# Two transformer blocks on one core: filler matmuls in the routings, one more weight slot, a reordered last expert and later lambda steps

## The chip, the core and the metric

The kernel runs on one core of a Trainium2 chip, as one program. The metric is the device time of that program in microseconds (us). The core's engines, each with a queue of its own, are TensorE (PE, matmuls; PEld is its loading of weights), VectorE (DVE), ScalarE (ACT), GpSimd (POOL) and SyncE (SP), which issues most transfers. All transfers share 16 DMA engines.

## The reference

The input is one sequence of 256 tokens of width 1024, in f32. Block 1 scales and shifts a normalised x by vectors made from a condition (six of them, `cond @ ada_w`), mixes tokens with differential attention (8 heads, each the difference of two softmaxes, weighted by a number lambda), and adds a mixture of 16 experts. Block 2 conditions x in the same way, mixes tokens with a sparse attention (scores of an index choose keys by top-k) and an RWKV recurrence side by side, and adds a mixture of 32 experts. Cut to what the change touches:

```python
lam = exp(sum(lam_q1 * lam_k1)) - exp(sum(lam_q2 * lam_k2)) + lam_init
a = softmax(s1) - lam * softmax(s2)
...
g_idx = argmax(t @ w_rg + b_rg)                 # one group of experts per token
top_v, top_i = top_k(e_logits[g_idx], 2)        # two experts in it
hid = silu(t @ w_gate) * (t @ w_up) * gates     # for each expert
y = hid @ w_down
...
x = block2(block1(x))
```

Every expert has 1024 x 512 weights for gate and up and 512 x 1024 for down, 6 MB per expert, all of which are read.

## The kernel before, in words

Activations are held in on-chip memory with features on the partitions (`xT`, eight blocks of 128 features x 256 tokens). Large buffers come from a pool of 1 MB units, `c.un` (`raw()` takes one, `give()` returns it). Weights arrive through a `Stream` (L98): each `get` or `load` takes the oldest of its slots and issues one transfer of 1 MB on SP's queue; `size(n)` and `grow()` set how many units serve as slots. A transfer waits on SP until its slot has been read, and at most eight are in flight. SP's queue is in order, so a step that waits on it holds all later loads.

The text is written stage by stage; a scheduler then sets the order of instructions on every engine by its own estimates, and where the text says `keep_in_program_order`, it leaves an instruction's place. Stretches in which several chains run side by side (`weave`, L137) take steps from each in turn.

The stages, with the parts the change touches:

- **First projections and attention of block 1.** `load_late` (L212) brings four vectors of 64, and on DVE makes the product `lp` (L220) and its sums `ls` (L222), on ACT their exponential (L223), on DVE lambda (L226, L227). L405 is the product with the condition weights `ada_w`, `rsx` (L1363) a copy that PE waits for, L738 a copy in the attention.
- **Output projection and router.** `Project.rest` (L913) finishes the four quarters q of an output projection; each quarter gives two feature blocks of xT, by L926 on DVE. When a block is ready, `each(fb)` calls `Tokens.block` (L944), which transposes it to rows of tokens in the accumulator `acc` (L953 or L955), and multiplies it with the router's weights (L957). After blocks 3 and 7 ACT squares half of the rows and sums them (L961). `Tokens.rstd` (L963) adds the sums (L967) and finds 1/rms.
- **Routing.** `Route.slots` scales the logits, picks the group and two experts on DVE (L1042 to L1060) and ranks the tokens of each expert with small matmuls (L1063 to L1065). `count` (L1086, L1087) and `flag` (L1092, L1094) give `rfl`, whether an expert has more tokens than its place holds (64 in block 1, 32 in block 2). `Tokens.high` and `low` (L978, L986) round the rows to two parts.
- **Dispatch and experts.** `dispatch` (L1113 on, matmul L1135) gathers the tokens of a few experts. `experts` (L1254) loops over the experts: gate and up (L1213), the previous expert's `back()`, its down projection (L1222), gate factor and rounding (L1193 to L1197), and `add`, which scatters the result into `acc` (L1239 in block 1, L1249 in block 2). `slots_T` makes the scatter matrix, `hidden` the hidden layer (L1151 to L1163). The last expert is split in two halves q of columns (matmul L1297). `at` names steps that are done ahead of an expert: `general` (`overflow`, L1302 on) contains the path for more tokens than fit. It reads the flag into registers (L1309) and branches (L1310); the branch is not taken with these inputs. In both blocks it stands ahead of expert 1, and afterwards returns the unit `c.uxT` that it would need.
- **End.** `end(q)` (L2237) copies half q of `acc` on DVE and ACT and sends it to the output from SP and ACT.
- **Between the blocks**, block 2 copies `acc` to xT (L2079) and squares it (L2080). In block 2, L1644 and L1648 make the first products of the recurrence, L1915 and L1916 the top-k, L2003 and L2004 the attention's scores; L624 is the low part of a rounding; L719 turns a row of factors that L1937 spreads.

## Time and profile before

| what | us |
|---|---|
| median of three timed runs | 1311.84 |
| lowest and highest | 1310.52, 1313.15 |
| profiled execution | 1314.67 |
| its span | 1313.1 |
| PE, PEld busy | 1120.9 (85%), 684.6 (52%) |
| DVE, ACT, POOL busy | 587.0 (45%), 345.1 (26%), 101.9 (8%) |
| mean granted clock of PE | 0.94 |

The experts of block 1 lie between about 246 and 490 us, those of block 2 between about 857 and the end. Busy times are sums over the span; a share says nothing of whether an engine sets the end in a stage. An entry in brackets behind an instruction is the idle time of its engine just before it, with what ended it; the granted clock is the share of full speed that PE was given.

### The profile page before, as it was taken

The numbers are of one execution on the slowest core, as the hardware profiler recorded it, in microseconds if no ns is written. First come the engines' busy times: TensorE is split into PE (matmuls) and PEld (weight loads), VectorE is DVE, ScalarE is ACT, GpSimd is POOL, SyncE is SP. The second block draws the span as 40 slices with busy tenths as digits, with TensorE's granted clock in tenths as the row PEclk, the third lists the DMA queues.
The fourth block names the chain that finished last, engine by engine and source line by source line (L and its number), as shares of the span: only waits on it lengthen the run. The fifth ranks groups of instructions, "written<-read, shape, count | busy, mean of one in ns | idle before, by whom it ended". The sixth has DMA issues, their size and how long they took to land. (4 is left out here: it accounts for less than half of the span.)

```text
span 1313.1 us, 19778 instructions
## 1 busy us (share of the span) xinstructions
PE 1120.9 (85%) x8050; PEld 684.6 (52%) x8050; DVE 587.0 (45%) x1435; ACT 345.1 (26%) x676; POOL 101.9 (8%) x115
## 2 busy tenths in 40 slices
PE   5899978799999987988899999799877786787775
PEld 2777768444444335886678779744322232232222
DVE  4568762423222237677676767443322132222112
ACT  3334441212111114552334324222211121111111
POOL 2521110100000004001410100000000000000000
PEclk7899987799999995998999999899998899989988
DMA  8777767699999912332055588679999999999995
GB/s 301 292 263 266 293 267 287 257 411 422 422 421 420 421 66 74 149 128 97 33 169 194 186 317 306 243 304 421 421 423 422 421 422 422 421 422 422 422 421 240
DMA packets 60513, 404.04 MB, mean 308 GB/s; under 512 B 7328, under 2 KB 7584, under 8 KB 14464
## 3 DMA queue, kind: packets, MB, share of 16 engines
q1 hardware_dynamic: 58464, 400.58, 76.1%
q10 hardware_dynamic: 1824, 2.00, 0.5%
q8 instruction: 65, 1.06, 0.3%
q0 software_dynamic: 128, 0.13, 0.2%
q14 instruction: 32, 0.26, 0.1%
HBM read 401.64 MB, written 1.05 MB: 307 GB/s over the span
## 5 line engine op out<-in xcount | busy, mean ns | idle before, releaser
L1213 PE MATMUL a<-u,u 128*32 128x512 f32 (+1 forms) x1480 | 288.4, 610 | 38.8 <-DMA u<-in_expert_w_up 24.8
L1193 DVE SCALAR_TENSOR_TENSOR gs<-a,gc,gt 128x512 f32<-128x512 f32 (+1 forms) x50 | 37.6, 751 | 377.2 <-PE a L1222 366.4
L1213 PEld LDWEIGHTS a<-u,u 128*32 128x32 f32 (+1 forms) x1480 | 70.9, 120 | 181.6 <-issue 113.9
L1222 PE MATMUL a<-u,hid 128*32 128x512 f32 (+1 forms) x704 | 127.4, 622 | 36.7 <-DMA u<-in_expert_w_down 36.7
L679 PE MATMUL a<-u,u 128*128 128x256 f32 x656 | 142.9, 295 | 2.6 <-DVE u L624 2.6
L679 PE MATMUL a<-u,hi 128*128 128x256 f32 x640 | 136.9, 305 | 0.4 <-ACT u L1528 0.4
L1151 ACT COPY gs<-a 128x512 f32<-128x512 f32 x48 | 28.1, 585 | 337.0 <-PE a L1213 337.0
L679 PEld LDWEIGHTS a<-u,u 128*128 128x128 f32 x656 | 106.0, 196 | 12.6 <-issue 9.2
L1195 ACT CAST u<-gs 64x512 fp32r<-64x512 f32 x96 | 59.2, 616 | 198.9 <-DVE gs L1193 197.8
L679 PEld LDWEIGHTS a<-u,hi 128*128 128x128 f32 x640 | 101.0, 194 | 14.7 <-issue 9.3
L1222 PEld LDWEIGHTS a<-u,hid 128*32 128x32 f32 (+1 forms) x704 | 31.2, 119 | 112.2 <-issue 45.2
L1197 DVE TENSOR_TENSOR u<-gs,u 64x512 fp32r<-64x512 f32 x96 | 65.9, 686 | 27.2 <-ACT u L1195 25.3
L624 DVE TENSOR_TENSOR u<-u,hi 128x1024 fp32r<-128x1024 f32 x48 | 63.6, 1332 | 15.4 <-ACT hi L623 15.1
L623 ACT CAST hi<-u 128x1024 fp32r<-128x1024 f32 x48 | 49.8, 1047 | 75.0 <-PE a L679 68.8
L903 PE MATMUL a<-u,u 128*128 128x256 f32 x256 | 48.1, 307 | 6.6 <-DVE u L624 5.8
L624 POOL TENSOR_TENSOR u<-u,u 128x512 fp32r<-128x512 f32 (+1 forms) x22 | 43.1, 1975 | 135.1 <-ACT u L623 135.1
L1180 DVE CAST PT<-a 128x256 fp32r<-128x256 f32 x48 | 20.4, 424 | 63.2 <-PE a L1178 38.3
L1249 PE MATMUL acc<-u,PT 128*128 128x512 f32 x128 | 43.9, 456 | 5.2 <-DVE u L1197 3.6
L457 DVE SCALAR_TENSOR_TENSOR mvsum<-u,cond_c,mvsum 128x512 f32<-128x512 f32 x56 | 43.0, 768 | 11.6 <-DMA u<-in_ada_w 10.9
L1158 PEld LDWEIGHTS a<-sel,gs 128*128 128x128 f32 x256 | 34.3, 208 | 26.5 <-issue 25.5
L758 PE MATMUL e<-u,u 128*128 128x256 f32 x288 | 40.4, 307 | 5.5 <-ACT u L586 5.0
L623 ACT CAST u<-u 128x512 fp32r<-128x512 f32 (+1 forms) x52 | 40.9, 830 | 15.2 <-PE a L903 7.3
(445 smaller groups left out, 1555.1 us busy)
## 6 DMA issues: line engine op xcount, KB each, us to landing
u<-in_expert_w_up SPq DMA_DIRECT2D x93, 1024.0 KB, 19.7
u<-in_expert_w_gate SPq DMA_DIRECT2D x92, 1024.0 KB, 19.8
u<-in_expert_w_down SPq DMA_DIRECT2D x92, 1024.0 KB, 19.7
u<-in_ada_w SPq DMA_DIRECT2D x32, 1024.0 KB, 6.6
u<-in_w_in SPq DMA_DIRECT2D x19, 1024.0 KB, 4.8
u<-in_ada_w SPq DMA_DIRECT2D x32, 512.0 KB, 4.0
u<-in_attn_w_in SPq DMA_DIRECT2D x12, 512.0 KB, 8.7
u<-in_attn_w_in SPq DMA_DIRECT2D x6, 1024.0 KB, 7.0
```

What stands on the lines that cost most here:

```text
L457: V.scalar_tensor_tensor(out=mine[0], in0=w[:, k], scalar=cs[:, k:k + 1], in1=mine[0], op0=ALU.mult, op1=ALU.add)
L623: nc.scalar.copy(h[:, o], w[:, o])
L624: (nc.vector if e == "v" else nc.gpsimd).tensor_tensor(l[:, o], w[:, o], h[:, o].bitcast(F32), ALU.subtract)
L679: c.nc.tensor.matmul(ps, a[:, k, c0:c0 + n], b[:, k], start=k == 0 and i == 0, stop=k == kn - 1 and i == 2)
L758: T.matmul(p[:, j * S:(j + 1) * S], l, r, start=(h, j, k, n) == (0, 0, 0, 0), stop=(h, k, n) == (1, 3, 2), skip_group_check=True)
L903: self.c.nc.tensor.matmul(ps[:, j * S:(j + 1) * S], a[:, k, j * P:(j + 1) * P], b[:, k], start=k + j + i == 0, stop=k == KD - 1 and i == 2 ...
L1193: c.nc.vector.scalar_tensor_tensor(out=y[o], in0=py[o], scalar=gc[o], in1=gt[o], op0=ALU.mult, op1=ALU.mult)
L1195: c.nc.scalar.copy(yy[H2[q], q], y[H2[q]])
L1197: c.nc.vector.tensor_tensor(yy[H2[1 - q], q], y[H2[q]], yy[H2[q], q].bitcast(F32), ALU.subtract)
L1213: c.nc.tensor.matmul(pg[r:r + cap], xe[:, k0 + k, x0:x0 + cap], w[:, k, :], start=k0 + k < nk, stop=k0 + k >= KD - nk)
L1222: c.nc.tensor.matmul(py[r:r + cap], hT[:, f], w[:, f - f0, q * 512:(q + 1) * 512], start=f < nk, stop=f >= 4 - nk)
L1249: c.nc.tensor.matmul(acc[:, 2 * t + q], PT[:, t * P:(t + 1) * P], yy[:, q], start=False, stop=stop, skip_group_check=True)
```

## The change

- Lambda's product, sum and exponential are placed by the program's order.
- `rest` hands over blocks 4 and 5 in the middle of the last quarter's projection.
- `acc` becomes four tiles of one bank each. The squares of the second half are done in two parts, after blocks 5 and 7.
- `rstd` issues six matmuls, 128x512 in f32, whose result nobody reads.
- In block 2, `uxT` is given before the slots grow; `general` stands ahead of expert 30, and takes a slot back for `uxT`; ahead of expert 31 four slots are taken for the output copies.
- With `early`, expert 31's hidden layer comes before expert 30's return, and both halves' last matmuls before the adds of the halves.

```diff
@@ load_late
-    nc.vector.tensor_tensor(lp, lm[:, 0:2], lm[:, 2:4], ALU.mult)
+    own(nc.vector.tensor_tensor(lp, lm[:, 0:2], lm[:, 2:4], ALU.mult))
...
-    nc.vector.tensor_reduce(ls, lp, AX.X, ALU.add)
-    nc.scalar.activation(ls, ls, AF.Exp)
+    own(nc.vector.tensor_reduce(ls, lp, AX.X, ALU.add))
+    own(nc.scalar.activation(ls, ls, AF.Exp))
@@ Project.rest
-                run(self.part(q, ps, w, 0, 8))
+                run(self.part(q, ps, w, 0, 4))
+                for fb in (4, 5) if q == 3 else ():
+                    each(fb)
+                run(self.part(q, ps, w, 4, 8))
...
-            for fb in ((), (), (0, 1, 2, 3), (4, 5))[q]:
+            for fb in (0, 1, 2, 3) if q == 2 else ():
                 each(fb)
@@ Tokens.block
-            o = self.acc[:, 2 * t + q, k % 4 * P:(k % 4 + 1) * P]
+            o = self.acc[2 * t + q][:, k % 4 * P:(k % 4 + 1) * P]
...
-        if k % 4 == 3:
+        if k in (3, 5, 7):
+            o = slice(0, 512) if k == 3 else slice(0, 256) if k == 5 else slice(256, 512)
             for t in range(2):
-                c.nc.scalar.activation(self.u[:, :512], self.acc[:, 2 * t + q], AF.Square, accum_out=self.ss[:, t, q:q + 1])
+                c.nc.scalar.activation(self.u[:, o], self.acc[2 * t + q][:, o], AF.Square,
+                                       accum_out=self.ss[:, t, k // 2 - 1:k // 2])
@@ Tokens.rstd
-        V.tensor_tensor(v, self.ss[:, :, 0], self.ss[:, :, 1], ALU.add)
+
+        ps = bank(c)
+        for _ in range(6):
+            c.nc.tensor.matmul(ps, c.ones, self.u[:, :512], start=True, stop=True)
+        V.tensor_reduce(v.unsqueeze(2), self.ss, AX.X, ALU.add)
@@ experts
-        if hid is not None:
+        if hid is not None and not (early and e == NE - 1):
             out = back()
         PT, gc = slots_T(c, ep, slot[:, :, e:e + 1], gate[:, :, e:e + 1], cap)
-        hid = e, hidden(c, ep, pg, cap), PT, gc
+        hT = hidden(c, ep, pg, cap)
+        if early and e == NE - 1:
+            out = back()
+        hid = e, hT, PT, gc
...
-    add(*out)
+    if not early:
+        add(*out)
...
+    def last(q):
+        add(ys[q], PT, True, (q,))
+        end(q)
     for q in range(2):
...
-        add(gated(c, ep, py, gc, gt, (q,)), PT, True, (q,))
-        end(q)
+        if q:
+            c.ys.reverse()
+        ys.append(gated(c, ep, py, gc, gt, (q,)))
+        if not early:
+            last(q)
+    if early:
+        add(*out)
+        last(0)
+        last(1)
@@ block 1 and block 2
-    acc = c.e1.enter_context(tc.tile_pool(name="accp", bufs=1, space=PSUM)).tile([P, 4, 512], F32, name="acc")
+    acc = four_banks(c.e1.enter_context(tc.tile_pool(name="accp", bufs=1, space=PSUM)))
...
+def four_banks(pool):
+    return [pool.tile([P, 512], F32, name=f"acc{i}") for i in range(4)]
...
+        un.give(c.uxT)
         st.grow()
...
         def general():
+            st.size(len(st.slots) - 1)
+            c.uxT = un.raw()
             overflow(c, ep, fl_, "_2", 32, 32, (th_, tl_), slot, gate, add, c.gt2)
-            un.give(c.uxT)
-            st.grow()
...
-                f = c.xe[:, 512 * (2 * q + t):512 * (2 * q + t + 1)]
-                copy(f, acc[:, 2 * t + q])
+                f = c.un.raw()[:, :512]
+                copy(f, acc[2 * t + q])
                 dma.dma_start(out[0, t * P:(t + 1) * P, q * 512:(q + 1) * 512], f)
-        experts(c, "y", 32, (th_, tl_), slot, gate, add, 32, ep, c.gt2, {1: general}, end)
+        experts(c, "y", 32, (th_, tl_), slot, gate, add, 32, ep, c.gt2, {30: general, 31: lambda: st.size(len(st.slots) - 4)}, end, True)
```

The changed program's lines are shifted: its L960 and L962 are L955 and L957 of before, L977 are the six new matmuls, L1074 is L1063, L1233 is L1222, L1260 is L1249, L1318 is L1297, L1337 is L1309, L1672 is L1644, L721 is L719, L1965 is L1937.

In the following pieces rows that repeat the one ahead of them are left out. SP's queue at the start of block 2's experts, before: `xu` and `u` are slots, `rfl` is the flag.

```order
L128 DMA xu_7132<-in_expert_w_gate 128x2048 [waits DMASW0_49,SP_sequencer_49,DMASW1_49,DVE_sequencer_49,DMASW2_49,PE_sequencer_49,DMASW3_49,Activation_sequencer_49,DMAHW1_49,Pool_sequencer_49,PE_49]
L128 DMA u_7269<-in_expert_w_gate 128x2048 [waits DMAHW2_49,PE_49]
L128 DMA u_7270<-in_expert_w_up 128x2048 [waits DMAHW3_49,DVE_49]
L1309 TENSOR_LOAD rfl_7265 [waits PE_49,DVE_49,Activation_49,Pool_49]
L1309 ISA x2
L128 DMA xu_7132<-in_expert_w_gate 128x2048 [waits DMAHW4_49,DMAHW1_49,PE_49]
L128 DMA u_6849<-in_expert_w_up 128x2048 [waits DMAHW5_49,PE_49]
L1310 COMPARE_AND_BRANCH
```

And with the change:

```order
L128 DMA xu_7149<-in_expert_w_gate 128x2048 [waits DMASW0_49,SP_sequencer_49,DMASW1_49,DVE_sequencer_49,DMASW2_49,PE_sequencer_49,DMASW3_49,Activation_sequencer_49,DMAHW1_49,Pool_sequencer_49,PE_49]
L128 DMA u_7293<-in_expert_w_gate 128x2048 [waits DMAHW2_49,PE_49]
L128 DMA u_7295<-in_expert_w_gate 128x2048 [waits DMAHW3_49,DVE_49,PE_49]
L128 DMA u_7294<-in_expert_w_up 128x2048 [waits DMAHW4_49,DVE_49,PE_49]
L1337 TENSOR_LOAD rfl_7289 [waits PE_49,DVE_49,Activation_49,Pool_49]
L1337 ISA x2
L128 DMA xu_7149<-in_expert_w_up 128x2048 [waits DMAHW5_49,DMAHW1_49,PE_49]
```

Four loads stand ahead of the flag where three stood; the branch has left this place, and comes 160 rows later, with twelve loads behind it.

PE at the end of the program, before: `hid` is an expert's hidden layer, `PT` a scatter matrix.

```order
L1222 MATMUL a<-u_7270,hid 32x512 [waits DMAHW6_49,DVE_49]
L1222 MATMUL a<-xu_7132,hid 32x512 [waits DMAHW7_49]
L1158 MATMUL a<-sel,gs 128x64 [waits Activation_49]
L1249 MATMUL acc<-u_7267,PT 128x512 [waits DVE_49]
L1249 MATMUL acc<-u_7267,PT 128x512 [waits DVE_49]
L1297 MATMUL a<-u_6849,hid 32x512 [waits DMAHW0_49,DVE_49]
L1297 MATMUL a<-u_6850,hid 32x512 [waits DMAHW1_49,PE_49]
L1249 MATMUL acc<-u_7267,PT 128x512 [waits DVE_49]
L1249 MATMUL acc<-u_7267,PT 128x512 [waits Activation_49]
```

And with the change, where `acc` has four numbers:

```order
L1169 MATMUL a<-sel,gs 128x64 [waits Activation_49]
L1233 MATMUL a<-u_6866,hid 32x512 [waits DMAHW6_49,DVE_49,PE_49]
L1233 MATMUL a<-u_6867,hid 32x512 [waits DMAHW7_49]
L1318 MATMUL a<-u_6868,hid 32x512 [waits DMAHW0_49,DVE_49]
L1260 MATMUL acc_6723<-u_7291,PT 128x512 [waits DVE_49]
L1260 MATMUL acc_6724<-u_7291,PT 128x512 [waits DVE_49]
L1318 MATMUL a<-u_6869,hid 32x512 [waits DMAHW1_49]
L1260 MATMUL acc_6723<-u_7291,PT 128x512 [waits DVE_49]
L1260 MATMUL acc_6724<-u_7291,PT 128x512 [waits DVE_49]
```

The hidden layer of expert 31 (L1169, L1158 before) has moved ahead of expert 30's down projection, the scatters of expert 30 stand between the two halves, and the last scatter no longer waits for ACT.

PE in block 2, before: `b<-` are the first products of the recurrence, `grows` and L2003 belong to the attention.

```order
L719 MATMUL a<-ident,u_2728 128x128 [waits DVE_49]
L679 MATMUL a<-u_3690,hi_3806 128x256
L1644 MATMUL b<-u_4672,u_4403 64x128 x2
L1937 MATMUL a<-grows_4706,u_2728 128x256 [waits Activation_49]
L2003 MATMUL a<-u_3928 128x128 [waits DVE_49]
L1644 MATMUL b<-u_4672,u_4403 64x128 x7
L2003 MATMUL a<-u_3928 128x256 [waits DVE_49] x2
L1644 MATMUL b<-u_4672,u_4403 64x128 x15
L2019 MATMUL a<-ident,u_4156 128x128 [waits Pool_49] x2
```

And with the change:

```order
L681 MATMUL a<-u_3701,u_3817 128x256
L1672 MATMUL b<-u_4684,u_4415 64x128 [waits DVE_49]
L1672 MATMUL b<-u_4684,u_4415 64x128 x31
L721 MATMUL a<-ident,u_2740 128x128 [waits DVE_49]
L1965 MATMUL a<-grows_4718,u_2740 128x256 [waits Activation_49]
L681 MATMUL a<-u_3701,hi_3818 128x256 [waits PE_49]
```

The 32 products stand in one block ahead of the attention's factors.

## Rows read from the trace of the kernel before

**Rows 1.** Windows: us; busy (count) of PE, PEld, DVE, ACT, POOL; PEclk, DMA share, GB/s.

```profile
275.00:300.00 25.00, 24.88 (x143) 12.72 (x140) 7.75 (x19) 4.98 (x9) 0.00 (x0) 1.00 1.01 422
950.00:975.00 25.00, 18.38 (x122) 6.95 (x116) 6.78 (x16) 3.61 (x7) 0.00 (x0) 1.00 1.01 422
```

**Rows 2.** Chain that ended last, block 2's experts: start, duration, what.

```profile
938.46 1.97 PE a L1135 x16
...
1274.70 19.75 DMA xu<-in_expert_w_down
```

**Rows 3.** Timeline of the first projections: start, duration, engine, line, operation.

```profile
19.10 0.29 DVE L220 TENSOR_TENSOR lp<-lm 128x128 f32<-128x128 f32 x1 [5.63 <-DMA lm<-in_attn_lam_k]
...
20.10 3.64 PE L405 MATMUL a<-u,cond_c 128*32 128x512 f32 x16 [3.91 <-DVE rsx L1363]
...
20.95 0.20 PEld L405 LDWEIGHTS a<-u,cond_c 128*32 128x32 f32 x4 [0.66 <-DMA u<-in_ada_w]
```

**Rows 4.** Windows of 2 us in both routings, columns as in rows 1.

```profile
228.00:230.00 2.00, 0.00 (x0) 0.00 (x0) 1.29 (x8) 0.43 (x2) 0.00 (x0) 1.00 0.50 205
...
238.00:240.00 2.00, 2.00 (x12) 2.00 (x11) 2.00 (x6) 0.00 (x0) 0.00 (x0) 0.50 0.04 8
...
848.00:850.00 2.00, 0.01 (x1) 0.05 (x1) 1.76 (x15) 1.57 (x4) 0.00 (x0) 0.50 0.03 8
```

**Rows 5.** Timeline of the first routing and its dispatch.

```profile
224.90 0.88 DVE L926 SCALAR_TENSOR_TENSOR u<-a,mod,u 128x256 f32<-128x256 f32 x2 [7.61 <-PE a L903]
...
227.03 0.60 ACT L961 ACTIVATE u<-acc 128x512 f32<-128x512 f32 x1 [8.21 <-PE acc L955]
...
228.46 0.16 DVE L967 TENSOR_TENSOR tv<-u 128x2 f32<-128x2 f32 x1 [2.69 <-ACT u L961]
...
234.01 0.61 PE L1063 MATMUL a<-rA,tri 128*128 128x16 f32 x2 [6.73 <-DVE rA L1060]
...
237.02 5.86 PE L1135 MATMUL a<-pm,u 128*128 128x256 f32 x32 [0.69 <-DVE pm L1120]
...
237.12 2.72 DVE L986 SCALAR_TENSOR_TENSOR u<-acc,ty,u 128x512 fp32r<-128x512 f32 x4
...
242.71 3.60 PE L1447 MATMUL acc<-u,ident 128*128 128x512 f32 x8
```

**Rows 6.** Timeline of the second routing and its dispatch.

```profile
849.99 0.61 PE L1063 MATMUL a<-rA,tri 128*128 128x32 f32 x2 [7.77 <-DVE rA L1060]
...
852.42 2.72 DVE L986 SCALAR_TENSOR_TENSOR u<-acc,ty,u 128x512 fp32r<-128x512 f32 x4
...
855.90 1.49 DVE L1142 TENSOR_SCALAR u<-a,A2b,mod 128x256 f32<-128x256 f32 x3 [0.76 <-PE a L1135]
...
857.89 0.14 DVE L1094 TENSOR_SCALAR rfl<-rcm 128x1 int32<-128x1 f32 x1
...
861.15 0.33 SPq L128 DMA_DIRECT2D xu<-in_expert_w_gate  x1
```

**Rows 7.** Timeline of the program's end.

```profile
1299.19 3.74 PE L1297 MATMUL a<-u,hid 128*32 128x512 f32 x16
...
1305.13 0.74 PE L1249 MATMUL acc<-u,PT 128*128 128x512 f32 x2 [2.20 <-DVE u L1197]
...
1306.64 0.58 ACT L2237 COPY u<-acc 128x512 f32<-128x512 f32 x1 [1.57 <-DVE u L2237]
...
1307.27 1.22 PE L1249 MATMUL acc<-u,PT 128*128 128x512 f32 x2 [1.40 <-ACT u L2237]
...
1309.94 0.35 ACTq L2238 DMA_DIRECT2D out<-u  x1
```

**Rows 8.** Timeline of the block boundary, VectorE's first copies.

```profile
491.49 2.48 DVE L2079 COPY u<-acc 128x512 f32<-128x512 f32 x4 [0.59 <-PE acc L1239]
```

**Rows 9.** Timeline of block 2 before its attention's scores.

```profile
631.13 1.10 PE L1644 MATMUL b<-u,u 64*64 64x128 f32 x30
...
633.13 0.75 DVE L1648 TENSOR_TENSOR u<-b,u 128x256 f32<-128x256 f32 x2
```

More of the change, by code (lines that the diff above doesn't have):

```diff
@@ L218, in load_late @@
         nc.gpsimd.dma_start(lm[:, i, :], I[nm].partition_broadcast(P))
+    own = c.tc.keep_in_program_order
     lp = tp.tile([P, 2, 64], F32, name="lp")
-    nc.vector.tensor_tensor(lp, lm[:, 0:2], lm[:, 2:4], ALU.mult)
+    own(nc.vector.tensor_tensor(lp, lm[:, 0:2], lm[:, 2:4], ALU.mult))
     ls = tp.tile([P, 2], F32, name="ls")
-    nc.vector.tensor_reduce(ls, lp, AX.X, ALU.add)
-    nc.scalar.activation(ls, ls, AF.Exp)
+    own(nc.vector.tensor_reduce(ls, lp, AX.X, ALU.add))
+    own(nc.scalar.activation(ls, ls, AF.Exp))
     c.lam = cp.tile([P, 1], F32, name="lam")
@@ L941, in __init__ @@
         self.u = c.un.raw()
-        self.ss = self.u[:, 512:516].rearrange("p (t q) -> p t q", t=2)
+        self.ss = self.u[:, 512:518].rearrange("p (t q) -> p t q", t=2)
     def block(self, k):
@@ L1238, in add @@
                 fb = 4 * q + b
-                c.nc.tensor.matmul(acc[:, fb // 2, (fb % 2) * S:(fb % 2 + 1) * S], yy[:, q, b * P:(b + 1) * P], PT,
+                c.nc.tensor.matmul(acc[fb // 2][:, (fb % 2) * S:(fb % 2 + 1) * S], yy[:, q, b * P:(b + 1) * P], PT,
                                    start=False, stop=stop, skip_group_check=True)
@@ L1248, in add, with experts @@
             for t in range(2):
-                c.nc.tensor.matmul(acc[:, 2 * t + q], PT[:, t * P:(t + 1) * P], yy[:, q],
+                c.nc.tensor.matmul(acc[2 * t + q], PT[:, t * P:(t + 1) * P], yy[:, q],
                                    start=False, stop=stop, skip_group_check=True)
     return add
-def experts(c, pfx, NE, tok, slot, gate, add, cap, ep, gt, at={}, end=lambda q: None):
+def experts(c, pfx, NE, tok, slot, gate, add, cap, ep, gt, at={}, end=lambda q: None, early=False):
     nc, st = c.nc, c.st
@@ L1446, in block1 @@
         for b in range(4):
-            nc.tensor.matmul(acc[:, b], c.ident, fl(xT[:, 2 * b:2 * b + 2]), start=True, stop=False, skip_group_check=True)
+            nc.tensor.matmul(acc[b], c.ident, fl(xT[:, 2 * b:2 * b + 2]), start=True, stop=False, skip_group_check=True)
         split_rows(c)
@@ L1456, in block1 @@
         un.give(uoh, uol, c.uys, c.xe)
-    return acc.rearrange("p a (b s) -> p (a b) s", b=2)
+    return acc
 def lin_block(c, name, x, sink):
@@ L2186, in block2 @@
         pl = stack.enter_context(tc.tile_pool(name="pl2", bufs=1, space=PSUM))
-        acc = stack.enter_context(tc.tile_pool(name="accp2", bufs=1, space=PSUM)).tile([P, 4, 512], F32, name="acc")
+        acc = four_banks(stack.enter_context(tc.tile_pool(name="accp2", bufs=1, space=PSUM)))
         c.banks.append((pe, 1))
```

7 lines of the change are left out of this document (4 added, 3 removed).

## The prediction, made before the changed kernel ran

> **What bounds the kernel now.** I read the table of windows first, for the limit of each stage. In [rows 1] the experts of block 1 show TensorE (PE) busy 24.88 of 25 us, so the sixteen experts are bound by PE; those of block 2 show PE busy 18.38 of 25, yet DMA share 1.01 at 422 GB/s: the thirty-two are bound by weight loading. A step is therefore judged by its stage: before 863 us by the instruction chain, afterwards by when the weight stream starts and how soon the output leaves once the stream has ended.
>
> The chain of waits agrees: up to the end of the last experts it hops from load to load, [rows 2] being one, 19.75 us from issue to landing; since eight are in flight, one load lands every 19.75 / 8 = 2.47 us. The other row there is a dispatch in the middle of these experts: 16 matmuls in 1.97 us, 0.123 us each. That is the price at the higher of TensorE's two clock levels, 2.4 GHz; both routings pay more, below.
>
> **The change part by part.** The sum is made against the profiled execution (1314.67 us, span 1313.1). It stands 2.83 us above the median 1311.84 of the three timed runs, so the changes are taken off the median.
>
> *Lambda's first steps, -0.3.* The product `lp` sat on VectorE (DVE) until lambda's vectors had landed, 5.63 us idle, and only then came the copy `rsx`, for which PE waited 3.91 us [rows 3]. Now `rsx` goes first. Not all of the 3.91 returns: PE's second group of weights arrives at 20.95 in any case [rows 3], and the work after it, half of 3.64 us, would end near 22.9 instead of 23.74: -0.8. Lambda's two large steps (0.29 us for the row shown, the second as long by estimate) go into the attention, among DVE's work there; I charge +0.5, bounds 0 and +0.9. No DMA moves with them.
>
> *Fillers in both routings.* While DVE finds experts, PE idles 6.73 us in the first routing and 7.77 in the second [rows 5, 6]. The granted clock falls during it, from 1.00 to 0.50, and is still 0.50 while the dispatch runs [rows 4]: 32 matmuls in 5.86 us, 0.183 each [rows 5]. The six extra matmuls have the shape of L1447, whose four instructions (8 records) took 3.60 us [rows 5], 0.90 each: 5.4 us. They can start when the squares are done; from there to the rank matmul stand 234.01 - 228.46 = 5.55 us, so they fit with 0.15 to spare. (228.46 is where DVE takes the squares' sums up.) Afterwards the dispatch, at the middle experts' 0.123, takes 3.94: -1.9. A bound lies on it: its low halves need DVE's L986, which ends at 239.84, so eight matmuls end no earlier than 240.8 against 242.88, which leaves that -1.9 whole. The rank matmuls before it, 0.61 for the first two records [rows 5], give about -0.4, an estimate. In the second routing L986 ends at 855.14 and L1142 waited just 0.76 longer for PE [rows 6], so the dispatch can give at most 0.76; I take -0.6, and -0.4 for the ranks.
>
> *Blocks of x moved ahead of the last projection half.* Before, feature blocks 4 and 5 hid DVE's L926 (0.88 us for two) [rows 5]. Moved forward, they no longer do: half of the 0.88 and a handover, +0.6 for each routing. The final squares shrink from 512 to 256 columns; two of 0.60 each [rows 5] lose about a third: -0.4. Net +0.2 each, bounds -0.2 and +0.9. First routing: -1.9 - 0.4 + 0.2 = **-2.1**. Second: -0.6 - 0.4 + 0.2 = **-0.8**; it counts since the expert-overflow flag `rfl` (857.89) releases SyncE's queue: the next load is issued at 861.15, 3.26 later [rows 6].
>
> *One more slot, -2.5.* SyncE now issues a fourth load before it waits for the flag. The DMA engines have run dry by then (8 GB/s at 848 to 850 [rows 4]), so that 1 MB costs nothing: 1.05 MB / 422 GB/s = 2.5 us less of a stage that runs at the full rate until its end. Bounds 0 (the load is not ready in time) and -2.5.
>
> *The end of the program, -3.7.* Before, the last projections end at 1299.19 + 3.74 = 1302.9 [rows 7], both halves of the columns are gated only afterwards, and one accumulator tile makes the two scatters and four copies take turns: PE waits 1.40 us for a ScalarE (ACT) copy of the first half before it adds the second [rows 7], and the last output leaves at 1309.94. Now expert 31's hidden layer precedes expert 30's return, and the last matmul of the second half ends near 1302.0. That end is an estimate: the load of [rows 2] lands at 1294.45, the last of all two later, 1294.45 + 2 x 2.47 = 1299.4; its eight matmul records take half of 3.74, 1.9, and I add 0.7 for expert 30's scatters, which now stand just before them. From there 2.2 for gating and rounding (as from 1302.9 to the first scatter at 1305.13), 0.74 for two scatters and 0.58 for the ACT copy [rows 7] give 1305.5; I add 0.7 for handovers and for the first half's copies on the same engines, so 1306.2 where 1309.94 stood: -3.7. Bounds -2.5 (half of the overlap lost) and -5.
>
> *Four accumulators at the block boundary, -0.6.* DVE's first copy starts 0.59 after it became free, waiting for PE's last scatter [rows 8]; the first bank is complete earlier. Bounds 0 and -1.
>
> *General path late, 0.* At expert 1 its branch lay in a stage that the stream bounds; at expert 30 it still does, and PE idles 6.6 of 25 us there [rows 1]. If that cover were gone the price would be what the flag cost the queue, 3.26 (second rival).
>
> *The scheduler's new order in block 2, 0.* The 32 matmuls L1644 now all come before the two L719 and the attention products behind them. At 1.10 us for 30 [rows 9] they take 1.2. On DVE their eight L1648 (0.375 each by its row, 3.0) come before rather than after attention's scores. What they delay there they free later; bounds -2 and +4.2.
>
> Sum: -0.3 - 2.1 - 0.8 - 2.5 - 3.7 - 0.6 = **-10.0**, so 1311.84 - 10.0 = **1301.8 us**.
>
> **The rivals.**
>
> *The clock falls all the same.* For: 1.2 us of idle (228.46 less 234.01 - 6.73) remains before the fillers, and more follows around the ranks. Against: at 228 to 230, when the fillers would begin, the clock is still 1.00 [rows 4]. Lost are 1.9 + 0.4 + 0.6 + 0.4 = 3.3: 1305.1 us. The Trainium skill ("TensorE: Matmul & The Clock Gate", Part 1) says that half rate is the default, that activity releases it, and that the moment varies from run to run; by that rule a gain of this kind could appear in one execution and be missing in the next. The rows of before, a single execution, agree with the fall and cannot show the scatter.
>
> *The late branch breaks the tail.* It comes with twelve loads left, and slots are taken from the stream at experts 30 and 31. If the branch holds SyncE as the flag did, 3.26 us [rows 6], with no further load to make it up: 1305.1. Against: eight loads in flight last 19.75 us.
>
> *Block 2's order costs.* L1644 and L1648 delay the attention chain by 1.2 + 3.0 = 4.2: 1306.0; if DVE's other moved steps (top-k, splits) add as much again, 1310.2, no measurable change.
>
> *Slower: the fillers hold up the routing.* They stand in PE's queue ahead of the rank matmuls. At 0.90 each they are hidden by 0.15; above 0.92 each the first routing waits for them. If they run at half the clock, 1.8 each, 10.8 us, the first rank matmul comes 10.8 - 5.55 = 5.2 late, the second routing's 4.2 late (its idle time is 1.0 longer), and the 3.3 are lost too: -10.0 + 5.2 + 4.2 + 3.3 = +2.7, 1314.5. Against: 1.00 at the moment of their start.
>
> **How the numbers follow.** Forecast 0.60; clock falls 0.13; late branch 0.09; order of block 2 0.11 (0.06 of it the milder price, 0.05 the double); fillers slower 0.07. Measurements of this kernel tell apart about 0.2%, 2.6 us. Faster: 0.60 + 0.13 + 0.09 + 0.06 = 0.88; same 0.05; slower 0.07. For the range, the low bounds of tail, boundary and order (-1.3, -0.4, -2), with the attention free of lambda (-0.5) and the moved blocks (-0.4 each) give about 1296.5; the high end takes in the three faster rivals and a little of their sum: 1308.5.
>
> **What would show it.** Right: PE busy with L977 matmuls between squares and ranks, clock 1.00 through both dispatches, at about 0.12 us per matmul; four loads issued before the flag; DMA at 422 GB/s to the end and 10 rather than 13.7 us between the last landing (near 1299.5 before) and the end of the span; `rsx` copied before 19 us. Wrong: granted clock 0.50 in a dispatch, rank matmuls that wait for PE's own queue, holes in the DMA share after expert 30, or a stretch between 500 and 830 us that is longer by more than 4 us.

## The result and the profile after

The change made the kernel slightly slower. The median of eleven runs is 1322.54 us, against 1315.65 for eleven runs of the kernel before: 6.9 us by the medians. The ratio is 1.0064 (95% interval 1.0046 to 1.0081), by which it is 8.4 us: under 1%, but clear of noise. The prediction said 1301.8; of the 20.7 us between the two, 3.8 are the base, since it started from the median of three runs before, 1311.84.

The page of the profiled execution after, 1319.64 us (its span; busy time, share and instructions of each engine):

```profile
span 1318.1 us, 19835 instructions
...
PE 1140.0 (86%) x8074; PEld 689.6 (52%) x8074; DVE 583.6 (44%) x1435; ACT 347.2 (26%) x684; POOL 105.2 (8%) x115
```

The sums say little: PE is busy 19 us longer than before, at the same mean clock of 0.94. So I followed the same instruction in both traces, stage by stage. The table gives when each stage ends in the profiled executions.

| stage, and the instruction at which it ends (lines of before) | before | after | change of the stage | forecast |
|---|---|---|---|---|
| first projections, to the first L813 | 84.15 | 81.51 | -2.6 | -0.8 |
| attention, to the end of the last L858 | 199.69 | 201.81 | +4.8 | +0.5 |
| projection, routing 1, to the first L1213 | 246.24 | 246.15 | -2.2 | -2.1 |
| experts of block 1, to the first L1297 | 480.24 | 486.59 | **+6.4** | none |
| boundary, to the first L2079 | 491.49 | 497.78 | -0.1 | -0.6 |
| block 2, to the end of the last L903 | 838.72 | 852.52 | **+7.5** | 0 |
| routing 2, to the end of L1094 | 858.03 | 868.61 | -3.2 | -0.8 |
| weight stream, to the end of the last L1151 | 1292.11 | 1300.23 | -2.5 | -2.5 |
| end, to the end of the span | 1313.1 | 1318.1 | -3.1 | -3.7 |

Three stages became longer, by 18.7 us. The other six became shorter by 13.7, against 10.5 that I had forecast for them. The difference, +5.0, is that of these two executions; by the medians it is more. A stage's length in one execution also holds some luck of the clock, as the experiments show below.

**First projections.** The timeline after, answering to [rows 3] (start, duration, engine, line, operation, idle time before it):

```profile
15.94 0.42 DVE L1391 COPY rsx<-a 128x256 f32<-128x256 f32 x1 [2.22 <-PE a L556]
...
20.89 1.06 PE L407 MATMUL a<-u,cond_c 128*32 128x512 f32 x8 [1.86 <-DMA u<-in_ada_w]
```

`rsx` starts at 15.94 and PE's second group no longer waits for it. The last weights arrive at 20.89, and only one group of eight records (1.06) is left behind them, not the half of 3.64 that I had charged. Not all of the 2.6 is the change's: of the kernels below without lambda's pins, all but `best2` also reach the first L813 earlier than this execution of before, by 0.6 to 2.2 us.

**Attention.** What PE waited for between 100 and 205 us (line waited at, by whom, us in total, times, longest), after:

```profile
PE a L905 <- DVE u L626: 8.1, 1, 8.1
PE a L860 <- DVE on L852: 5.3, 2, 3.8
```

and before:

```profile
PE a L903 <- DVE u L624: 5.8, 1, 5.8
PE a L858 <- DVE on L850: 3.8, 1, 3.8
```

The same two waits are 2.3 and 1.5 us longer: 3.8 of the stage's 4.8.

**Experts of block 1.** L1204 (L1193 before) gates an expert's result once per expert. Its row after, near the end of the stage (line, engine, operation, count: duration in ns, first and last start):

```profile
L1204 DVE SCALAR_TENSOR_TENSOR gs<-a,gc,gt x3: 750/751/751, 453.0 to 483.0; 128x512 f32<-128x512 f32 x3
```

and before:

```profile
L1193 DVE SCALAR_TENSOR_TENSOR gs<-a,gc,gt x3: 750/751/751, 448.0 to 476.6; 128x512 f32<-128x512 f32 x3
```

Three starts are two periods: 30.0 / 2 = 15.0 us per expert after, 28.6 / 2 = 14.3 before. The first four periods are equal in both kernels, the next ten add up to +6.5: six are 0.3 to 0.7 longer, two are 2.1 longer and two 0.7 shorter. In PE's timeline one sees what an expert pays for. After:

```profile
383.95 2.30 PE L1233 MATMUL a<-u,hid 128*64 128x512 f32 x7
...
386.18 0.44 PE L1187 MATMUL a<-ident,gp 128*128 128x128 f32 x2
...
386.45 0.51 PE L1189 MATMUL a<-rgate,gp 128*128 128x1 f32 x4
...
386.89 1.94 PE L1233 MATMUL a<-u,hid 128*64 128x512 f32 x8
...
391.05 1.22 PE L1250 MATMUL acc<-PT,u 128*128 128x256 f32 x6 [0.64 <-DVE u L1208]
```

Before:

```profile
382.50 4.02 PE L1222 MATMUL a<-u,hid 128*64 128x512 f32 x15
...
386.94 0.38 PE L1176 MATMUL a<-ident,gp 128*128 128x128 f32 x2
...
388.73 0.74 PE L1239 MATMUL acc<-PT,u 128*128 128x256 f32 x4 [0.41 <-DVE u L1197]
...
389.31 0.50 PE L1178 MATMUL a<-rgate,gp 128*128 128x1 f32 x4
```

Before, the fifteen L1222 run as one piece, and the small groups L1176 and L1178 (L1187, L1189 after) come later, while PE would otherwise wait for DVE's gating: only 0.41 us of waiting is left ahead of the scatter L1239. After, they stand in the middle of the down projection; between its halves lie 386.89 - (383.95 + 2.30) = 0.64 us, DVE gets its result later, and PE then waits 0.64 instead of 0.41. That fits the usual period; the two that are 2.1 longer I didn't follow. Nothing in the diff touches these lines.

**Block 2.** The largest shift arises between 549 and 570 us. PE's timeline just before, after the change:

```profile
547.34 0.71 PE L1932 MATMUL a<-u 32*128 32x128 f32 x4 [0.81 <-DVE u L1977]
...
548.58 0.63 PE L527 MATMUL a<-u,ones 128*32 128x256 f32 x4 [0.54 <-ACT u L1935]
...
549.73 0.60 PE L535 MATMUL a<-c,npart 64*128 64x1 f32 x4 [0.52 <-DVE npart L531]
```

Windows after (columns as in rows 1):

```profile
546.00:548.00 2.00, 1.19 (x9) 0.84 (x7) 2.00 (x3) 1.91 (x4) 0.00 (x0) 1.00 0.00 0
552.00:554.00 2.00, 2.00 (x8) 1.38 (x7) 2.00 (x12) 0.84 (x2) 0.91 (x1) 0.50 0.54 147
550.00:575.00 25.00, 25.00 (x113) 20.43 (x114) 14.38 (x52) 10.88 (x19) 1.19 (x1) 0.66 0.21 81
```

and the kernel before in the last of these stretches:

```profile
550.00:575.00 25.00, 24.63 (x182) 21.75 (x182) 18.65 (x39) 17.32 (x27) 0.00 (x0) 1.00 0.31 110
```

Before, PE has 182 matmul records there at full clock. After, three short waits, none above 0.81 us, interrupt PE between 546 and 550; then the granted clock falls, and is 0.50 in all eight windows from 552 to 568, although PE is busy throughout. Over this stretch the lag behind the kernel before grows from 7.5 to 16.8 us; by 618 us it has come back to 10.9, and at 693 us it is 13.6.

**The routings** did what they should, nearly, in this execution. Windows after, answering to [rows 4]:

```profile
230.00:232.00 2.00, 2.00 (x4) 0.80 (x5) 1.65 (x11) 0.00 (x0) 0.00 (x0) 0.67 0.99 414
232.00:234.00 2.00, 2.00 (x4) 0.96 (x3) 1.68 (x14) 1.74 (x4) 0.00 (x0) 0.50 0.47 193
864.00:866.00 2.00, 2.00 (x18) 2.00 (x18) 2.00 (x4) 0.00 (x0) 0.00 (x0) 1.00 0.56 234
```

Timeline of routing 1, answering to [rows 5]:

```profile
229.92 7.11 PE L977 MATMUL a<-u,ones 128*128 128x512 f32 x12 [0.61 <-ACT u L967]
...
235.21 0.18 DVE L1071 TENSOR_SCALAR rA<-re 128x32 f32<-128x32 f32 x1
...
236.87 0.29 PE L1074 MATMUL a<-rA,tri 128*128 128x16 f32 x2
...
238.75 3.33 PE L1146 MATMUL a<-pm,u 128*128 128x256 f32 x26 [0.69 <-DVE pm L1131]
```

The fillers ran at a low clock for 4 us (0.67, 0.50) and so took 7.1 us instead of 5.4. `rA` was ready at 235.21 + 0.18 = 235.39, and the rank matmul came at 236.87: 1.5 late, which is the start of the rival "the fillers hold up the routing". But then the clock was up, and 26 dispatch matmuls took 3.33, 0.128 each. Routing 2, answering to [rows 6]:

```profile
861.06 0.33 SPq L128 DMA_DIRECT2D u<-in_expert_w_up  x1
...
866.52 1.44 DVE L1153 TENSOR_SCALAR u<-a,A2b,mod 128x256 f32<-128x256 f32 x3
...
868.47 0.14 DVE L1105 TENSOR_SCALAR rfl<-rcm 128x1 int32<-128x1 f32 x1
```

The fourth load stands at 861.06 ahead of the flag (868.47), and L1153 has no wait in front of it.

**The end**, answering to [rows 7]:

```profile
1305.15 1.91 PE L1318 MATMUL a<-u,hid 128*32 128x512 f32 x8 [1.49 <-DMA u<-in_expert_w_down]
...
1306.99 1.20 PE L1260 MATMUL acc<-u,PT 128*128 128x512 f32 x4
...
1308.12 1.91 PE L1318 MATMUL a<-u,hid 128*32 128x512 f32 x8
...
1312.73 1.22 PE L1260 MATMUL acc<-u,PT 128*128 128x512 f32 x2 [2.04 <-DVE u L1208]
```

The first half's matmuls wait for their load, the scatters of expert 30 stand between the halves, and ahead of the last scatter PE waits for DVE's rounding, no longer for ACT's copy.

### The profile page after: what moved, and what is told of

Same layout as the page of the kernel before. It is cut to its first block, busy times and chain, and to the rows that moved or that the text cites. A ratio compares the mean times of both kernels' runs of the same rounds, so it can differ in the third digit from the quotient of the medians.

```text
span 1318.1 us, 19835 instructions
## 1 busy us (share of the span) xinstructions
PE 1140.0 (86%) x8074; PEld 689.6 (52%) x8074; DVE 583.6 (44%) x1435; ACT 347.2 (26%) x684; POOL 105.2 (8%) x115
## 3 DMA queue, kind: packets, MB, share of 16 engines
q8 instruction: 65, 1.06, 0.3%
## 4 chain that ended last, share of the span: by engine, by line
PE 41%; DMA 30%; DVE 7%; ACT 1%; issue 1%; POOL 0%; SPq 0%; DVEq 0%; ACTq 0%
DMA u<-in_expert_w_gate 11%; DMA u<-in_expert_w_down 11%; PE a L1224 10%; PE a L681 10%; DMA u<-in_expert_w_up 7%; PE a L1233 5%; PE a L905 2%; PE acc L1250 2%; DVE u L626 1%; DMA u<-in_ada_w 1%; DVE u L1208 1%; PE a L1318 1%; PE b L1751 1%; DVE mvsum L459 1%; PE a L1187 1%
## 5 line engine op out<-in xcount | busy, mean ns | idle before, releaser
L1224 PE MATMUL a<-u,u 128*32 128x512 f32 (+1 forms) x1480 | 292.4, 616 | 36.8 <-DMA u<-in_expert_w_up 24.7
L1204 DVE SCALAR_TENSOR_TENSOR gs<-a,gc,gt 128x512 f32<-128x512 f32 (+1 forms) x50 | 37.5, 751 | 288.1 <-PE a L1233 280.1
L1233 PE MATMUL a<-u,hid 128*32 128x512 f32 (+1 forms) x704 | 130.4, 623 | 32.3 <-DMA u<-in_expert_w_down 32.1
L681 PE MATMUL a<-u,hi 128*128 128x256 f32 x640 | 142.2, 313 | 0.0
L681 PEld LDWEIGHTS a<-u,u 128*128 128x128 f32 x656 | 106.9, 196 | 14.4 <-issue 8.7
L681 PEld LDWEIGHTS a<-u,hi 128*128 128x128 f32 x640 | 104.8, 200 | 16.2 <-issue 11.5
L1233 PEld LDWEIGHTS a<-u,hid 128*32 128x32 f32 (+1 forms) x704 | 30.5, 119 | 101.6 <-DMA u<-in_expert_w_down 44.2
L626 DVE TENSOR_TENSOR u<-u,hi 128x1024 fp32r<-128x1024 f32 x48 | 63.9, 1339 | 21.0 <-ACT hi L625 20.8
L626 POOL TENSOR_TENSOR u<-u,u 128x512 fp32r<-128x512 f32 (+1 forms) x22 | 43.6, 2001 | 126.8 <-ACT u L625 126.8
L1169 PEld LDWEIGHTS a<-sel,gs 128*128 128x128 f32 x256 | 35.1, 212 | 27.3 <-issue 25.6
L1260 PE MATMUL acc<-u,PT 128*128 128x512 f32 x128 | 44.7, 462 | 3.1 <-DVE u L1208 3.1
L905 PEld LDWEIGHTS a<-u,u 128*128 128x128 f32 x256 | 40.3, 214 | 9.4 <-DVE u L626 8.3
```

The costliest lines, as they stand in the source:

```text
L626: (nc.vector if e == "v" else nc.gpsimd).tensor_tensor(l[:, o], w[:, o], h[:, o].bitcast(F32), ALU.subtract)
L681: c.nc.tensor.matmul(ps, a[:, k, c0:c0 + n], b[:, k], start=k == 0 and i == 0, stop=k == kn - 1 and i == 2)
L905: self.c.nc.tensor.matmul(ps[:, j * S:(j + 1) * S], a[:, k, j * P:(j + 1) * P], b[:, k], start=k + j + i == 0, stop=k == KD - 1 and i == 2 ...
L1169: nc.tensor.matmul(pt[:, f * w:(f + 1) * w], gs[:, f * P:(f + 1) * P], fl(c.sel), start=True, stop=True)
L1204: c.nc.vector.scalar_tensor_tensor(out=y[o], in0=py[o], scalar=gc[o], in1=gt[o], op0=ALU.mult, op1=ALU.mult)
L1224: c.nc.tensor.matmul(pg[r:r + cap], xe[:, k0 + k, x0:x0 + cap], w[:, k, :], start=k0 + k < nk, stop=k0 + k >= KD - nk)
```

## The experiments

All ratios are to the kernel before, on the same chip, with 95% intervals. Line numbers are those of each kernel, off by one or two.

What moves instructions in stages that the diff doesn't touch can be read from the order of the rows in the traces. In block 1's experts and in block 2 it is one line, `ps = bank(c)` ahead of the fillers: with the counter alone moved (`bank_only` against before), 82 of PE's 1128 matmul records in the experts and 250 of 3234 in block 2 stand outside the longest order that both have in common; with the whole change but the counter moved back (`turn` against before) none and 16. `bank` (L385) hands out accumulator banks in turn, by a counter `c.turn`. One call more, and every later group of matmuls gets another bank than before, and the scheduler orders anew. In the attention the pins of lambda's steps move rows (`only_lam` against before: 55 on DVE, 13 on PE), the counter one. The runs had to show whether these orders cost the time.

### The bank counter alone, and taken back

`bank_only` is the kernel before with the counter moved once in each routing, without any filler; `turn` is the change with the counter moved back.

```diff
 # bank_only, in rstd of the kernel before
+        c.turn += 1
         V.tensor_tensor(v, self.ss[:, :, 0], self.ss[:, :, 1], ALU.add)
 # turn, in rstd of the change
             c.nc.tensor.matmul(ps, c.ones, self.u[:, :512], start=True, stop=True)
+        c.turn -= 1
```

> The kernel of before with nothing but the bank counter moved on by one in each routing; no work is added or removed. Theory (the rotation alone makes the loss): experts of block 1 at 15.0 us each, block 2 longer by about 7 us, the whole 10 to 14 us above before, ratio 1.008 to 1.011. Rival (the fillers or the four tiles make it): 1.000.

> The change, with the counter that hands out the accumulator banks put back by one after the fillers, so that every later matmul group gets the bank it had before; the six fillers stay. Theory (the shifted rotation of banks makes the scheduler order block 1's experts and block 2 anew, and this costs 6.4 and 7.5 us in the trace of the change): experts of block 1 back at 14.3 us each from 15.0, and the whole 12 to 14 us below the change, near 0.996 of before. Rival (four accumulator tiles or the fillers' time itself slow these stages): no faster than the change, 1.006.

Measured: `bank_only` 1.0105 (1.0080 to 1.0131), median 1328.37 against 1314.55, so **+13.8 us without one instruction more**. `turn` 0.9973 (0.9956 to 0.9989), 1311.17, which is 11.4 below the change. The window of block 2 in `bank_only`:

```profile
550.00:575.00 25.00, 25.00 (x110) 20.22 (x110) 14.39 (x52) 10.74 (x18) 1.19 (x1) 0.64 0.19 69
```

and in `turn`:

```profile
550.00:575.00 25.00, 24.63 (x182) 21.84 (x181) 18.64 (x43) 17.64 (x29) 0.00 (x0) 1.00 0.31 104
```

and `turn`'s gating row in block 1's experts:

```profile
L1205 DVE SCALAR_TENSOR_TENSOR gs<-a,gc,gt x3: 751/751/751, 450.1 to 478.7; 128x512 f32<-128x512 f32 x3
```

With the counter moved, the low clock is there (0.64); with it restored, the clock is 1.00 and the period is 14.3 again ((478.7 - 450.1) / 2), as in every profiled execution with the old order; the three with the new order have 15.0. In the profiled executions of this study, this stretch had 0.64 to 0.71 in the three kernels with the new order (the change, `bank_only`, `no_lam`), and 1.00 in before and the ten others. The bank counter is the cause, in both directions.

The length of block 2 as a whole doesn't show this: in `turn` it is still 8.5 us longer than before, in `turn_nolam` below 11.1. So I split the stage at one row that all kernels have, the first L2113 on ACT (L2146 in `turn`), in before and in `turn`:

```profile
658.24 0.57 ACT L2113 ACTIVATE u<-a 128x512 f32<-128x512 f32 x1
...
659.16 0.58 ACT L2146 ACTIVATE u<-a 128x512 f32<-128x512 f32 x1
```

Up to it, from the first L2079, before takes 166.75 us, and `turn` 0.9 more; the three kernels with the new order take 6.8 (`no_lam`), 7.5 (the change) and 10.6 (`bank_only`) more, the ten with the old order between 0.3 less and 1.1 more. From it to the end of the stage all lie within 2.4 us of before, those with the new order too, except `turn` (7.6 longer) and `turn_nolam` (10.2), whose clock fell there in the profiled execution; `turn`:

```profile
760.00:780.00 20.00, 16.88 (x200) 11.75 (x201) 12.87 (x22) 2.87 (x6) 0.00 (x0) 0.91 0.82 305
```

Before has 1.00 in this stretch. `turn_nolam` has 0.77 from 780 to 800, and `t_noearly`, which has the same order on every engine up to routing 2, has 1.00: there the fall belongs to the execution, not to the order.

### Lambda's pins

```diff
 # no_lam: the change without the pins; only_lam: the kernel before, with the pins alone
-    own(nc.vector.tensor_tensor(lp, lm[:, 0:2], lm[:, 2:4], ALU.mult))
+    nc.vector.tensor_tensor(lp, lm[:, 0:2], lm[:, 2:4], ALU.mult)
...
-    own(nc.vector.tensor_reduce(ls, lp, AX.X, ALU.add))
-    own(nc.scalar.activation(ls, ls, AF.Exp))
+    nc.vector.tensor_reduce(ls, lp, AX.X, ALU.add)
+    nc.scalar.activation(ls, ls, AF.Exp)
```

> The change without the fixed place of lambda's first steps. The order of every engine in block 1's attention is then that of before; elsewhere it is the change's. In the trace of the change the first projections come 2.9 us earlier, but by the end of the attention it is 2.1 us late. Theory (the new order of the attention costs about 5 us): the attention ends near 0 against before, and the whole comes out about 2 us below the change, ratio to before near 1.005. Rival (the 5 us are the scatter of one execution, and the pinned place gains 2.9): about 3 us above the change, 1.009.

> The kernel of before with lambda's three steps pinned as in the change, and nothing else. Theory (the pin brings the first projections forward, but the attention's new order on VectorE makes TensorE wait at its output transposes and before its last projection): first projections 2 to 3 us earlier, end of the attention 2 to 3 us later than before, whole 1.002 to 1.003. Rival (the loss in the attention was the scatter of two executions): 0.998.

Measured: `no_lam` 1.0048 (1.0025 to 1.0071), 1320.95; `only_lam` 1.0023 (1.0003 to 1.0044), 1314.71. PE's waits in the attention, `only_lam`:

```profile
PE a L904 <- DVE u L625: 8.1, 1, 8.1
PE a L859 <- DVE on L851: 5.2, 2, 3.8
```

The waits follow the pins, whatever else is in the kernel: 8.1 and 5.2 or 5.3 in the three kernels that have them; 5.3 to 6.2 and 3.7 or 3.8 in the eleven without. The length of the attention alone wouldn't show it: it is 4.7 to 5.8 us above before with the pins, but also 2.7 to 5.9 in four kernels without them (`turn_nolam`, `t_fill4`, `best1`, `best2`), each with a stretch at a lower clock than before, and -0.1 to +0.6 in the other six. In `only_lam` the front gains 3.2 us to the first score and the attention ends 1.4 later than before. So the pins lose, by the medians 1.6 us (the change against `no_lam`, where the intervals overlap), 2.3 (`only_lam` against before) and 5.0 (`turn` against the next kernel, where they don't). Which of the moved steps on DVE makes L626 late wasn't tried.

`only_lam` also corrects a reading of mine: it has the old order at the end, and its last projections are

```profile
1296.65 2.24 PE L1298 MATMUL a<-u,hid 128*32 128x512 f32 x16
```

2.24 us, where [rows 7] have 3.74. The kernel before happened to run its end at a low clock in the profiled execution, and 1.5 of the 3.1 us gained at the end come from that; the granted clock at the start of these matmuls was 0.50 there and 1.00 in `only_lam`.

### What is left without both: the rest of the change

`turn_nolam` has both edits, `turn`'s and `no_lam`'s. `nolam_nofill` is the change without pins, and without the fillers and their bank.

```diff
 # nolam_nofill
-        ps = bank(c)
-        for _ in range(6):
-            c.nc.tensor.matmul(ps, c.ones, self.u[:, :512], start=True, stop=True)
```

> Both: bank counter put back and lambda's steps free. What is left of the change is fillers, moved blocks, four accumulators, the extra slot, the late general path and the reordered end. Theory (the two new orders cost 5 and 14 us, the rest does what was forecast): about 9 us below before, 0.993. Rival (these parts cost something themselves): 1.000 or above.

> The change with lambda's steps free and without the six filler matmuls and their bank, so that the bank rotation is that of before. Theory (the fillers hold the clock through the dispatches): granted clock 0.50 in both dispatches again, 2 to 3.5 us above the version with fillers and restored rotation, ratio 0.994 to 0.995. Rival (the gain in the routings comes from the moved blocks and squares alone): 0.992 as with fillers.

Measured: `turn_nolam` **0.9923** (0.9896 to 0.9950), median 1306.14; `nolam_nofill` 0.9980 (0.9963 to 0.9998). By its ratio the first is 10.1 us faster than before; my terms without lambda's sum to -9.7. Routing 1 in `turn_nolam`:

```profile
226.00:246.00 20.00, 17.78 (x112) 13.74 (x111) 11.60 (x57) 5.56 (x16) 0.00 (x0) 1.00 0.42 166
```

and of `nolam_nofill`:

```profile
226.00:246.00 20.00, 12.85 (x64) 10.51 (x64) 11.99 (x59) 5.64 (x14) 0.00 (x0) 0.74 0.32 128
```

With fillers the granted clock is 1.00 through routing 1, without them 0.74, as in before; in routing 2 (846 to 866 us) it is 1.00 and 0.77. But the fillers don't hold it in every execution. `t_noearly` and `t_nogen` below have the same order as `turn_nolam` on every engine through routing 1, and in both the clock fell in its dispatch. Dispatch of `turn_nolam`, then of `t_nogen` with its window:

```profile
241.72 3.33 PE L1147 MATMUL a<-pm,u 128*128 128x256 f32 x26 [0.83 <-DVE pm L1132]
...
235.19 4.83 PE L1147 MATMUL a<-pm,u 128*128 128x256 f32 x26 [0.83 <-DVE pm L1132]
236.00:238.00 2.00, 2.00 (x14) 2.00 (x13) 2.00 (x4) 0.00 (x0) 0.00 (x0) 0.61 0.59 156
```

Of the nine kernels with six fillers, the clock stayed at 1.00 through routing 1 in five, and through routing 2 in five; in the four without fillers it was 0.50 in the dispatch of both. The difference of the two ratios, 0.0057, is 7.5 us; the two come from different groups of runs, and the intervals leave 3 to 12. The terms that hang on the fillers were 3.3 together. In the traces the two routings are 4.6 us shorter in `turn_nolam` than in `nolam_nofill`, and 2.3 in `t_noearly`, where the clock fell.

The profile of `turn_nolam` fell on its slowest execution (1317.73; the others 1301.47 to 1308.93): the clock was 0.80 between 90 and 115 us there, where `no_lam` and before have 1.00, and 0.77 between 780 and 800.

### How many fillers

```diff
 # t_fill4: turn_nolam with
-        for _ in range(6):
+        for _ in range(4):
```

> Bank rotation restored, lambda free, four fillers instead of six in each routing. In the change the first rank matmul of routing 1 comes 1.4 us after VectorE's result, behind the sixth filler. Theory (four still hold the clock, and no longer delay): ranks 1.4 us earlier in routing 1, ratio 0.991. Rival (with 2 us more of idle time the clock falls): granted clock 0.50 in a dispatch and 0.994.

Measured: 0.9946 (0.9924 to 0.9968). In routing 2:

```profile
848.00:850.00 2.00, 2.00 (x10) 2.00 (x11) 2.00 (x5) 0.00 (x0) 0.00 (x0) 0.50 0.84 352
```

In this execution four fillers held the clock at 1.00 through routing 1, and not through routing 2. Six lost it in routing 2's dispatch too, in three profiled executions (`t_noearly`, `t_nogen`, `best2`). So one execution can't tell four from six, and neither can the time, which isn't told apart from `turn_nolam`'s.

### Blocks 4 and 5

```diff
 # best1: turn_nolam, moved only in block 2's projection, "wob"; t_noeach: moved in neither
-                for fb in (4, 5) if q == 3 else ():
+                for fb in (4, 5) if q == 3 and self.name == "wob" else ():
...
-            for fb in (0, 1, 2, 3) if q == 2 else ():
+            for fb in ((), (), (0, 1, 2, 3), () if self.name == "wob" else (4, 5))[q]:
```

> Bank rotation restored, lambda free, fillers kept, but feature blocks 4 and 5 handed over after the last projection as before. As forecast blind the move costs 0.2 us per routing net with its squares: 0.992. By the trace of the change it brings about 1.6 us in the second routing: between the end of the projection and the scaling of the logits 1.6 us more, ratio 0.9935 to 0.994.

> Bank rotation restored, lambda free, feature blocks 4 and 5 moved ahead in block 2 alone. By the traces the move costs 1.0 us in the first routing and brings 0.8 in the second: ratio 0.9910 to 0.9915. Rival (the two are within the scatter): 0.992.

Measured: `t_noeach` 0.9919 (0.9893 to 0.9946), `best1` 0.9934 (0.9910 to 0.9959). In the traces the move costs routing 1 about 1.0 us (it gains 3.2 without the move, 2.2 with it) and brings routing 2 about 0.9 (from the last L903 to the logits -0.7 without, -1.6 with). The two cancel, and times can't tell these three kernels apart.

### The end and the slot

```diff
 # t_noearly: turn_nolam without the last argument True of block 2's experts
 # t_nogen: turn_nolam, with
-        {30: general, 31: lambda: st.size(len(st.slots) - 4)}
+        {1: general, 31: lambda: st.size(len(st.slots) - 4)}
```

In `t_nogen`, `general` gives `uxT` back only after expert 1, as before.

> Bank rotation restored, lambda free, but the last expert in the order of before (hidden layer after the previous expert's return, each half added before the next is projected); four accumulators and separate output units stay. As forecast blind the reordered end is worth 3.7 us: ratio 0.995. By the traces, in which the end of before also shows 1.7 us of half clock that other executions of the same order lack, it is worth 1 to 2: 0.9935.

> Bank rotation restored, lambda free, but the general path ahead of expert 1 and its unit given back only there, as before. Forecast: the load missing ahead of the flag costs 2.5 us: ratio 0.994 to 0.9945, three loads before the flag. Rival (the late branch costs about as much as the slot brings): 0.992, no change.

Measured: `t_noearly` 0.9942 (0.9922 to 0.9962), `t_nogen` 0.9959 (0.9936 to 0.9982). Neither interval is clear of `turn_nolam`'s, so the times alone prove nothing. The traces: without `early` the end gains 1.1 us over before (last L1151 to last scatter) where `turn_nolam` gains 3.0. Its last matmuls:

```profile
1292.51 2.51 PE L1319 MATMUL a<-u,hid 128*32 128x512 f32 x16
...
1297.36 2.07 PE L1261 MATMUL acc<-u,PT 128*128 128x512 f32 x4 [2.34 <-DVE u L1209]
```

One group of 16 and 2.34 us of waiting for DVE, instead of two groups with scatters between. Its clock was at 0.50 just before them, which costs it some of this: the old order at full clock (`only_lam`, `bank_only`) needs 14.7 us from the last L1151 to the end of the last scatter, the new one 13.2 to 13.7, before 16.4. The slot's 2.5 us shows in the stage table: -2.5 after, and only -0.2 in `t_nogen` from the flag to the last L1151, -0.6 and -0.4 in `bank_only` and `only_lam`, so about 2 us are the slot's.

### A way to keep both of lambda's gains, a miss

If lambda's vectors came earlier, no pin would be needed. `best2` is `best1` with

```diff
-        nc.gpsimd.dma_start(lm[:, i, :], I[nm].partition_broadcast(P))
+        nc.scalar.dma_start(lm[:, i, :], I[nm].partition_broadcast(P))
```

> As the one before, and lambda's four vectors are fetched from ScalarE's queue instead of GpSimd's, which issues them only at 8.6 us. Theory (the copy that the first projections wait for no longer stands behind a product that waits for data until 19.1 us, and the attention keeps its order): first projections 1.5 to 2.9 us earlier and kept to the end: 0.989 to 0.990. Rival (the transfers now delay ScalarE's first steps or other loads): 0.991 or above.

Measured: 0.9959 (0.9941 to 0.9977). Timeline of its first projections:

```profile
6.77 0.35 ACTq L218 DMA_DIRECT2D lm<-in_attn_lam_q  x1
...
19.41 0.29 DVE L222 TENSOR_TENSOR lp<-lm 128x128 f32<-128x128 f32 x1 [8.56 <-DMA lm<-in_attn_lam_k]
...
23.55 0.42 DVE L1392 COPY rsx<-a 128x256 f32<-128x256 f32 x1 [0.93 <-PE a L556]
```

The transfers are issued from 6.77 on, yet DVE's product waits for the last of them until 19.41, as in [rows 3] (19.10). In this kernel's order the chain that leads to the copy stands behind the product as well: `rsx` comes at 23.55.

## Why the prediction was wrong

**The step that failed** is "The scheduler's new order in block 2, 0", with its bounds of -2 and +4.2. It measured +7.5 (6.4 in `no_lam`, 9.4 in `bank_only`), all of it in the first half of the stage. I had priced the moved instructions (L1644, L1648) by their durations and taken the rest as neutral. Where those stand, between 618 and 693 us, the lag grows by 2.7, within my bounds. But 9.3 arise earlier, from 549 to 570, at three short waits that the new order opens and the low clock that follows them; 5.9 come back in between. The rival "Block 2's order costs" named the stage, with 4.2 and 8.4, but neither cause nor place; the forecast's own sign of being wrong, a stretch between 500 and 830 us longer by more than 4, came.

**The same cause had a second place that has no term at all**: the experts of block 1, +6.4. I had read that PE is busy 24.88 of 25 us there [rows 1] and gave the order no term, as if a stage bound by PE were indifferent to it. It isn't, where the 0.41 us that it does wait depends on which small group stands in the gap. Both places come from one `bank(c)` line: `bank_only` gives +13.8 us by the medians, where the two stages give 6.4 + 7.5 = 13.9 in the change (6.4 + 9.4 in `bank_only`'s own profile, less 2.4 elsewhere).

**Lambda, -0.3**: the attention was mis-sized. It took 4.8 instead of 0.5, since I counted only DVE's own time for the late steps and not what is queued behind them. The front gave 2.6 instead of 0.8, but 1.5 in `turn`, and kernels without the pins are 0.6 to 2.2 earlier than before there too, so what the pins themselves bring isn't shown to better than 1 or 2 us.

**Right in size**: the slot (-2.5 against -2.5) and, partly by luck, routing 1 (-2.2 against -2.1). Within routing 1 the fillers' margin of 0.15 was too thin: the rank matmul came 1.5 late in this execution, and the ranks and the dispatch gave that back. The same six fillers ran at 0.67 and 0.50 here and at 1.00 in `turn_nolam`. In `no_lam`, `t_noearly` and `t_nogen` the clock fell in the dispatch, as the rival "The clock falls all the same" has it, and routing 1 gained 0.9 to 1.0. That fits the rule of the Trainium skill that the forecast had weighed ("TensorE: Matmul & The Clock Gate", Part 1), by which the moment varies from run to run.

**Routing 2**, -3.2 against -0.8, was too small: I had capped the dispatch at the 0.76 us for which L1142 waited, but DVE's own work ahead of it also came sooner: from the rank matmul to L1142 were 5.91 us [rows 6] and are now 866.52 - 862.09 (the start of L1074) = 4.43, and the moved blocks brought 0.9 where I charged 0.2. Where the clock fell in this dispatch (`t_noearly`, `t_nogen`, `best2`), the gain was 2.1 or 2.2.

**The end**, -3.1 against -3.7, is right in mechanism, but about half of it is the low clock in the execution of before. The forecast's 1.9 us for the last eight records came out (1.91) by luck: it was half of a row at low clock, while the change ran them at 1.00, where the old order takes 2.24 for all sixteen. The **boundary** gave 0.1, and the four accumulators' -0.6 isn't seen. It gave 2.0 in `turn`, but also in `only_lam`, which has one accumulator: in both the sixteen last projections of block 1 took 5.42 us at a clock of 1.00, against 6.97 before, where the clock was 0.50 at their start.

**The general path late** cost nothing that a run shows.

Together: -10.1 (`turn_nolam`) + 13.8 (the counter) + 1.6 to 5.0 (the pins) = +5.3 to +8.7, and the change measured +8.4. The versions `turn_nolam`, `t_noeach` and `best1` (0.992 to 0.993) are faster than both kernels, and not told apart from one another.

## What to carry to other kernels

Before inserting filler or probe work, look at what it takes from shared counters and rotations (banks, buffers, slots): one call can re-order a program hundreds of microseconds later, and giving the turn back costs nothing. Compare the order of the instructions in stages that the diff doesn't touch, part by part; if they moved, the stage needs a term with a range of its own, also where one engine is busy all the time. A step that is pinned later costs what is queued behind it, not its duration. Before a stage's change is laid to an edit, look at the same stage in other kernels that have the same order there: single executions differed by 6 us in the attention and by 8 in the second half of block 2.
